# Down projection, last two blocks: 192 tokens first, then 128, with the first tokens' norm and outputs among the products

## The chip, the cores and the metric

The kernel runs on one NeuronCore of a Trainium2 chip. The metric is the device time of one execution in microseconds. Times below come from three timed runs and from one profiled execution of the kernel before; trace times are counted from the start of the profiled span.

## What is computed

One layer of a streaming encoder, for 256 prompt tokens and 64 sample tokens together (320 columns). Only its end matters here, the down projection of the feed-forward part, a norm per token, and the residual:

```python
def rmsnorm(x, g):
    y = xf * lax.rsqrt(jnp.mean(xf * xf, axis=-1, keepdims=True) + EPS)
    return (y * g).astype(x.dtype)

gate, up = jnp.split(gu, 2, axis=-1)
x = x + rmsnorm((jax.nn.silu(gate) * up) @ w_down, g_post_ffn)
```

The sum of squares of a token runs over all 2048 channels, so no output of a token can be scaled before the last of its 2048 channels is there.

## The kernel before

Channels lie on the 128 partitions and tokens along the free dimension, so the 2048 channels are 16 blocks of 128 (`KB`), numbered 0 to 15, and a block's values are a tile of 128 x 320. All float32 products are made from three products of rounded parts (type `F32R`): weight high part by activation high part, weight high by activation low, weight low by activation high. `load_split` (L218) loads a piece of weights by a DMA from SyncE's queue (L207), ScalarE rounds it to its high part `whi` (L214), and VectorE subtracts to get the low part `wlo` (L215). `whi` and `wlo` have three buffers each (`wsp`), and the loaded weights `w` three (`wst`). A cast to `whi` can start when the high-part products of three pieces before have been made; a load can start when the subtraction of three pieces before is done.

The down projection runs in four quarters of the 5632 hidden channels (`q`, L1154), each of 11 blocks of 128. For each quarter and each output block `n`, `block_matmul` (L222) takes the 11 hidden blocks as two pieces of 6 and 5 (768 and 640 weight columns): per piece the products with `gh` and `gl` (L230, L231), then the low-part products (L234). That is 33 products of 128 x 320 per block, each with its own 128 x 128 weights. Blocks 0 to 14 are added into `y` after each quarter (L1183); block 15 stays in a PSUM bank of its own through all four quarters (`held_y`, named `psy`, L1153 and L1187). In the last quarter each block's squares are added into `acc` (L1022, L1024) and `y` is multiplied by the gain (L1186).

After the last product of block 15 its squares are taken from PSUM (L1189). `rstd` (L251) adds `acc` and these squares over the partitions by products with a column of ones, which put the 320 sums on partitions (three overlapping ranges of 128 tokens, 12 records of TensorE, since plain float32 takes two passes), and takes the power -0.5 on GpSimd (L262). `rstd_rows` (L265) transposes the result back over 128 partitions (`psb`). Then the outputs follow in the order of `PLAN_Y` (L1194): VectorE multiplies one or two blocks by the row (L1220), and x is added in one of three ways: "P", two accumulating products with the identity on TensorE and a copy by ScalarE (L1150, L1229, L1230), "G" on GpSimd (L1222), "V" on VectorE (L1224). Each step ends with a DMA from SyncE's queue (L1213), in the order of the plan.

Instructions of each engine run in the order in which a scheduler laid them down at build time. `high_priority` moves instructions forward in that order, and `issue_after` ties one behind another.

Of the kernel before, what the change touches and what calls it, by code (L numbers as in the profile page):

```python
# [100 lines left out]
def trunk_kernel(ctx, tc, ins, outs):  # L101
# [1046 lines left out]
    def residual(k, pool, alone=False):  # L1148
        fin[k] = pool.tile([P, 512], F32, tag=pool.name[-1], name="fin")
        PE.matmul(fin[k][:, 0:T], cv("ident"), x1[:, k, :], start=True, stop=alone)  # L1150

    it = 0
    held_y = ps_g.tile([P, 512], F32, tag="g", name="psy")  # L1153
    for q in range(NQ):  # L1154
        gh = [act.tile([P, T], F32R, tag=f"bh{j}", name=f"gh{j}") for j in range(8)]
        for i in range(2):
# [16 lines left out]
        def gx(k):  # L1173
            return gh[k], gl[k]

        for n in range(KB - 1):
            psd = ps_p.tile([P, 512], F32, tag="p", name="psdn")
            block_matmul(psd[:, 0:T], ins["w_down"][q, n], gx, (6, 5))
            with tc.high_priority(offset=PRI_E):
                if q == 0:  # L1180
                    S.copy(y[:, n, :], psd[:, 0:T])
                else:
                    V.tensor_tensor(y[:, n, :], y[:, n, :], psd[:, 0:T], ALU.add)  # L1183
                if q == NQ - 1:
                    square_acc(n, y[:, n, :])
                    S.activation(y[:, n, :], y[:, n, :], AF.Identity, scale=pv("g4", n))  # L1186
        block_matmul(held_y[:, 0:T], ins["w_down"][q, KB - 1], gx, (6, 5), q == NQ - 1, q == 0)  # L1187
    with tc.high_priority(offset=PRI_E):
        last = square_acc(KB - 1, held_y[:, 0:T])  # L1189
        S.activation(y[:, KB - 1, :], held_y[:, 0:T], AF.Identity, scale=pv("g4", KB - 1))  # L1190
    nc.sync.dma_start(outs["ffn"], nffn)


    PLAN_Y = "P0 P1 G0809 P0203 G1011 P0405 G1213 P0607 V1415"  # L1194
    banks = [(ps_t, 0), (ps_t, 1), (ps_g, 2), (ps_g, 3), (ps_g, 4)]

    def residuals(n, mm):
        with tc.issue_after(mm.ins):
            for _ in range(n):
                pool, k = banks.pop(0)  # L1200
                residual(k, pool)

    rr, mm = rstd([acc, last], ps_p, lambda i, mm: residuals(2 * i, mm))
    rb3, mm = rstd_rows(rr, ps_p)
    residuals(3, mm)

    sent = None

    def out(k, n, sent):
        with ExitStack() as e:  # L1210
            if sent is not None:
                e.enter_context(tc.issue_after(sent.ins))
            return nc.sync.dma_start(outs["y"][:, k:k + n, :], y[:, k:k + n, :])  # L1213

    for step in PLAN_Y.split():
        how, ks = step[0], step[1:]
        n = 2 if len(ks) == 4 else 1
        k = int(ks[:len(ks) // n])
        yy = y[:, k:k + n, :]
        V.tensor_tensor(yy, yy, rb3.unsqueeze(1).to_broadcast((P, n, T)), ALU.mult)  # L1220
        if how == "G":
            G.tensor_tensor(yy, yy, x1[:, k:k + n, :], ALU.add)  # L1222
        elif how == "V":
            V.tensor_tensor(yy, yy, x1[:, k:k + n, :], ALU.add)  # L1224
        else:
            for kk in range(k, k + n):
                if kk not in fin:
                    residual(kk, (ps_t, ps_g)[kk % 2])
                PE.matmul(fin[kk][:, 0:T], cv("ident"), y[:, kk, :], start=False, stop=True)  # L1229
                S.copy(y[:, kk, :], fin[kk][:, 0:T])  # L1230
        sent = out(k, n, sent)
    pb.close()


# [79 lines left out]
```

## Time and profile before

| what | value |
|---|---|
| median of three runs | 1500.84 us (1497.14 to 1501.93) |
| profiled execution, its own time | 1498.26 us |
| its span, first to last instruction | 1496.5 us |
| outside the span | 1.76 us |
| TensorE busy, share of the span | 99% |
| weight loads (PEld) busy, share of the span | 98% |
| VectorE, ScalarE, GpSimd busy | 67%, 48%, 15% |
| mean granted TensorE clock | 0.998 |
| DMA traffic | 224.22 MB, mean 150 GB/s |

The page gives busy times per engine. TensorE's matmul ends are modelled and overlap, so the distance from one product's start to the next one's start is the better measure of its price; in a merged row of the timeline it is the row's length less one instruction's duration, divided by the count less one. A row of the timeline reads: start, length, engine, line, operation, output and inputs, shape, count, and in brackets how long the engine stood idle before it and on whom it waited.

### The profile page before, as it was taken

What the parts mean: (1) busy time and instruction counts of PE and PEld (TensorE: products, weight loads), DVE (VectorE), ACT (ScalarE), POOL (GpSimd) and SP (SyncE); (2) the same over time, 40 slices, a digit from 0 to 9 for tenths busy, and PEclk for the clock granted to TensorE, in tenths of its full rate; (3) what the DMA queues carried; (4) which work ended last, traced back from release to release, by engine and by line L of the source; (5) the groups of instructions that cost most, each with busy time, mean ns of one, the idle gap of its engine ahead of it and who ended that gap; (6) DMA issues with size and microseconds to landing.
All of it is one profiled execution on the core that took longest, in us unless ns stands there. A gap on an engine that the chain in (4) does not pass through costs nothing.

```text
span 1496.5 us, 27233 instructions
## 1 busy us (share of the span) xinstructions
PE 1480.7 (99%) x10609; PEld 1459.7 (98%) x10610; DVE 998.4 (67%) x1840; ACT 723.7 (48%) x1305; POOL 226.4 (15%) x390
## 2 busy tenths in 40 slices
PE   9999999999999999999999999999999999999998
PEld 8999899989999999999999999999999999999997
DVE  6779886979989678766335666445666545656554
ACT  7664556554544656544434444334444333444453
POOL 0011001120010000332002222002223101223101
PEclk9999999999999999999999999999999999999999
DMA  8435453444434744444554444454444455444453
GB/s 297 134 128 160 137 157 120 131 143 144 130 106 142 226 146 141 154 143 130 154 166 154 149 151 137 138 159 162 152 155 138 136 149 171 154 147 150 131 151 118
DMA packets 98281, 224.22 MB, mean 150 GB/s; under 512 B 18792, under 2 KB 39528, under 8 KB 98152
## 3 DMA queue, kind: packets, MB, share of 16 engines
q1 hardware_dynamic: 98008, 222.45, 47.4%
q8 instruction: 83, 1.36, 0.4%
q14 instruction: 46, 0.38, 0.1%
q10 hardware_dynamic: 144, 0.03, 0.0%
HBM read 215.33 MB, written 7.12 MB: 149 GB/s over the span
## 4 chain that ended last, share of the span: by engine, by line
PE 82%; DVE 9%; ACT 3%; DMA 2%; issue 2%; POOL 1%; ACTq 0%; DVEq 0%; POOLq 0%
PE psu L234 13%; PE psu L231 13%; PE psu L230 13%; PE psdn L230 7%; PE psdn L231 6%; PE psdn L234 6%; DVE wlo L215 3%; PE psq L230 3%; PE psq L231 3%; PE psq L234 3%; PE psu L1107 1%; ACT whi L214 1%; DVE cvt L560 1%; PE ps_first L395 1%; DMA w<-in_w_out 1%
## 5 line engine op out<-in xcount | busy, mean ns | idle before, releaser
L214 ACT CAST whi<-w 128x1024 fp32r<-128x1024 f32 (+2 forms) x440 | 412.9, 940 | 488.4 <-PE psu L231 169.4
L215 DVE TENSOR_TENSOR wlo<-w,whi 128x1024 fp32r<-128x1024 f32 (+2 forms) x440 | 477.3, 1085 | 196.5 <-ACT whi L214 124.7
L231 PE MATMUL psu<-lo,whi 128*128 128x320 f32 x1344 | 397.0, 309 | 0.0
L230 PE MATMUL psu<-hi,whi 128*128 128x320 f32 x1344 | 397.0, 309 | 0.0
L231 PEld LDWEIGHTS psu<-lo,whi 128*128 128x128 f32 x1344 | 252.3, 188 | 0.0
L230 PEld LDWEIGHTS psu<-hi,whi 128*128 128x128 f32 x1344 | 252.3, 188 | 0.0
L234 PE MATMUL psu<-hi,wlo 128*128 128x320 f32 x1344 | 224.4, 309 | 0.0
L234 PEld LDWEIGHTS psu<-hi,wlo 128*128 128x128 f32 x1344 | 204.0, 188 | 0.0
L231 PE MATMUL psdn<-gl,whi 128*128 128x320 f32 x660 | 195.9, 310 | 0.0
L1140 POOL COPY nffn<-fbuf 128x2 f32<-128x2 f32 x88 | 101.5, 1153 | 586.9 <-DVE fbuf L1138 583.7
L1138 DVE TENSOR_TENSOR fbuf<-psu,rb 128x256 f32<-128x256 f32 x88 | 37.4, 425 | 168.9 <-PE psu L234 168.9
L230 PE MATMUL psdn<-gh,whi 128*128 128x320 f32 x480 | 142.8, 309 | 0.0
L231 PEld LDWEIGHTS psdn<-gl,whi 128*128 128x128 f32 x660 | 123.9, 188 | 0.3
L230 PE MATMUL psq<-hh,whi 128*128 128x320 f32 x352 | 106.2, 315 | 0.0
L231 PE MATMUL psq<-hl,whi 128*128 128x320 f32 x352 | 104.1, 309 | 0.0
L230 PEld LDWEIGHTS psdn<-gh,whi 128*128 128x128 f32 x480 | 90.1, 188 | 0.0
L234 PE MATMUL psdn<-gh,wlo 128*128 128x320 f32 x480 | 89.9, 309 | 0.0
L234 PEld LDWEIGHTS psdn<-gh,wlo 128*128 128x128 f32 x480 | 75.3, 188 | 0.0
L230 PEld LDWEIGHTS psq<-hh,whi 128*128 128x128 f32 x352 | 66.1, 188 | 0.3
L231 PEld LDWEIGHTS psq<-hl,whi 128*128 128x128 f32 x352 | 66.1, 188 | 0.2
L560 DVE SCALAR_TENSOR_TENSOR cvt<-ub,par,cvt 128x320 f32<-128x320 f32 x120 | 65.3, 545 | 0.2
L1183 DVE TENSOR_TENSOR y<-y,psdn 128x320 f32<-128x320 f32 x45 | 22.0, 488 | 58.9 <-PE psdn L234 58.9
(357 smaller groups left out, 2479.5 us busy)
## 6 DMA issues: line engine op xcount, KB each, us to landing
w<-in_w_up SPq DMA_DIRECT2D x176, 512.0 KB, 3.6
w<-in_w_in SPq DMA_DIRECT2D x88, 512.0 KB, 3.9
w<-in_w_down SPq DMA_DIRECT2D x64, 384.0 KB, 3.2
w<-in_w_down SPq DMA_DIRECT2D x64, 320.0 KB, 2.9
w<-in_w_out SPq DMA_DIRECT2D x32, 320.0 KB, 3.3
w<-in_w_out SPq DMA_DIRECT2D x16, 384.0 KB, 3.1
w<-in_w_first SPq DMA_DIRECT2D x6, 512.0 KB, 6.5
wtp<-wsp SPq DMA_DIRECT2D x4, 640.0 KB, 5.8
```

The costliest lines, as they stand in the source:

```text
L214: S.copy(hi[:, 0:width], w[:, 0:width])
L215: V.tensor_tensor(lo[:, 0:width], w[:, 0:width], hi[:, 0:width].bitcast(F32), ALU.subtract)
L230: tick(PE.matmul(ps, wh, xh, start=(first and k0 + j == 0), stop=False))
L231: tick(PE.matmul(ps, wh, xl, start=False, stop=False))
L234: tick(PE.matmul(ps, lo[:, j * P:(j + 1) * P], xh, start=False, stop=(final and k0 + j == nk - 1)))
L395: tick(PE.matmul(ps, w, xh, start=(k == 0 and wt is hi), stop=(k == KB - 1 and wt is lo)))
L560: return lambda: V.scalar_tensor_tensor(acc, x, w, acc, ALU.mult, ALU.add)
L1107: PE.matmul(pss[i][:, 0:T], wt[:, o:o + P], x, start=(k == 0 and n == 0), stop=(k == KB - 1 and n == 2))
L1138: V.tensor_tensor(buf[:, 2:258], psu[:, 0:TP], rb2[:, 0:TP], ALU.mult)
L1140: G.tensor_copy(nffn[:, b, 0, :], buf[:, 256:258])
L1183: V.tensor_tensor(y[:, n, :], y[:, n, :], psd[:, 0:T], ALU.add)
```

## The change

The loop over the last quarter ends with block 13. `held_y` is gone: block 15 of the first three quarters is added into `y` like the others. For blocks 14 and 15 of the last quarter the four weight pieces are loaded and split first (`wl`), the last one into buffers of its own (`wsx`), and kept, because each is used twice: `part_products` makes the 33 products of a block for a range of tokens. The order in the program is block 14 and block 15 for tokens 0 to 191 (`ra`), then block 14 and block 15 for tokens 192 to 319 (`rz`). The sums of squares of the first tokens stand behind the 14th product of block 14's second part, and the transposes of their norm behind the 12th product of block 15's second part. Outputs are made by `out` for `ra` and then for `rz`, always two blocks at a time, eight steps each. The "P" step has one bank and two products for both blocks, 384 or 256 columns wide. The two blocks take 132 products in place of 66, 66 of them 128 x 192 and 66 of them 128 x 128. `then` ties each instruction behind the one before it on its engine; since `then` records them, most of the new instructions stand under its line, L1205.

```diff
-    held_y = ps_g.tile([P, 512], F32, tag="g", name="psy")
...
-        for n in range(KB - 1):
+        for n in range(KB if q < NQ - 1 else KB - 2):
...
-        block_matmul(held_y[:, 0:T], ins["w_down"][q, KB - 1], gx, (6, 5), q == NQ - 1, q == 0)
-    with tc.high_priority(offset=PRI_E):
-        last = square_acc(KB - 1, held_y[:, 0:T])
...
-    PLAN_Y = "P0 P1 G0809 P0203 G1011 P0405 G1213 P0607 V1415"
...
+    wsx = pb.enter_context(tc.tile_pool(name="wsx", bufs=1, reuse_waits="tile"))
+    for n in (n14, KB - 1):
+        for j0, nk in ((0, 6), (6, 5)):
+            src = ins["w_down"][NQ - 1, n][:, j0 * P:(j0 + nk) * P]
+            wl[n, j0] = load_split(src, nk * P, wsx if (n, j0) == (KB - 1, 6) else None)
...
+    def part_products(n, pool, r, between={}):
...
+                        then(PE, PE.matmul, ps[:, r], w[:, j * P:(j + 1) * P], x[j0 + j][:, r], start=first,
+                             stop=(w is lo and j0 + j == QB - 1))
...
+            then(PE, PE.matmul, fin, cv("ident"), xx, start=True, stop=False)
+            then(PE, PE.matmul, fin, cv("ident"), yy, start=False, stop=True)
+            then(S, S.copy, yy, fin)
...
+    TA = 192
+    ra, rz = slice(0, TA), slice(TA, T)
...
+    with tc.high_priority(offset=PRI_E):
+        evict(n14, part_products(n14, ps_t, ra), ra)
+        sqa = evict(KB - 1, part_products(KB - 1, ps_t, ra), ra)
+        root = []
+        evict(n14, part_products(n14, ps_p, rz, {14: lambda: root.append(row_root([acc, sqa], oa))}), rz)
+        psd = part_products(KB - 1, ps_t, rz, {12: lambda: root.append(rows(root[0], oa, ps_p))})
+        out("G0809", ra, root[1])
+        sqz = evict(KB - 1, psd, rz)
+        out("G1011", ra, root[1])
+        rr = row_root([acc, sqz], oz)
+        for step in ("P0001", "P0203"):
+            out(step, ra, root[1])
+        scale = rows(rr, oz, ps_t)
+        for step in ("G1213", "P0405", "G1415", "V0607"):
+            out(step, ra, root[1])
+        for step in ("P0001", "G0809", "P0203", "G1011", "P0405", "G1213", "G1415", "V0607"):
+            out(step, rz, scale)
```

The built order of three engines shows where this lands. Numbers behind names tell buffers apart. The first place is TensorE at the seam of blocks 12 and 13 of the last quarter. Before, block 13 (`psdn_16426`, with the first weight piece `whi_16429`) follows block 12 whole:

```order
L234 MATMUL psdn_16375<-gp1_14146,wlo_16403 128x320
L230 MATMUL psdn_16426<-gh0_14137,whi_16429 128x320
L231 MATMUL psdn_16426<-gl0_14147,whi_16429 128x320
...
L234 MATMUL psdn_16426<-gp1_14146,wlo_16454 128x320
L230 MATMUL psdn_16477<-gh0_14137,whi_16480 128x320
L231 MATMUL psdn_16477<-gl0_14147,whi_16480 128x320
```

Now, on the same engine, block 13 is `psdn_16431` (pieces `whi_16434` and, not shown, `whi_16458`), and the 192 tokens of block 14 are `psdn_16510` (pieces `whi_16488` and `whi_16494`):

```order
L234 MATMUL psdn_16380<-gp1_14151,wlo_16408 128x320
L230 MATMUL psdn_16431<-gh0_14142,whi_16434 128x320
L231 MATMUL psdn_16431<-gl0_14152,whi_16434 128x320
L1205 MATMUL psdn_16510<-gh0_14142,whi_16488 128x192
...
L1205 MATMUL psdn_16510<-gh5_14147,wlo_16489 128x192
L230 MATMUL psdn_16431<-gh1_14143,whi_16434 128x320
...
L234 MATMUL psdn_16431<-gh5_14147,wlo_16435 128x320
L1205 MATMUL psdn_16510<-gh6_14148,whi_16494 128x192
```

The first piece of block 14 (18 narrow products) stands behind two products of block 13, its second piece (15) behind block 13's first piece, and block 13's second piece comes after it.

The second place is ScalarE's casts of the last weight pieces. Before, they stand in the order of their use: `whi_16453` is block 13's second piece, `whi_16480` and `whi_16504` are block 14's, `whi_16530` and `whi_16554` block 15's:

```order
L214 CAST whi_16453<-w_16451 128x640
L214 CAST whi_16480<-w_16478 128x768
L1022 ACTIVATE sq_16422<-y_7189 128x320
L1186 ACTIVATE y_7189<-y_7189,par_81 128x320
L214 CAST whi_16504<-w_16502 128x640
L214 CAST whi_16530<-w_16528 128x768
```

Now `whi_16458` is block 13's second piece, `whi_16488` and `whi_16494` are block 14's, `whi_16500` and `whi_16506` block 15's:

```order
L214 CAST whi_16458<-w_16456 128x640
L214 CAST whi_16488<-w_16486 128x768
L1022 ACTIVATE sq_16427<-y_7189 128x320
L1185 ACTIVATE y_7189<-y_7189,par_81 128x320
L214 CAST whi_16506<-w_16504 128x640
L214 CAST whi_16494<-w_16492 128x640
L214 CAST whi_16500<-w_16498 128x768
```

Block 15's second piece, the last one loaded, has moved ahead of block 14's second piece.

The third place is the end of VectorE's program. Before, `psb_16591` is the row of the norm:

```order
L1024 TENSOR_TENSOR acc_15811<-acc_15811,sq_16524 128x320
L261 TENSOR_SCALAR rr_16588<-pst_16577 128x3
L1220 TENSOR_TENSOR y_7189<-y_7189,psb_16591 128x320 x2
L1220 TENSOR_TENSOR y_7189<-y_7189,psb_16591 128x640 x7
L1224 TENSOR_TENSOR y_7189<-y_7189,x1_6308 128x640
```

Now `psb_16647` is the row of the first 192 tokens, `psb_16699` that of the others, and `psdn_16634` the last 128-token product of block 15:

```order
L1205 TENSOR_TENSOR y_7189<-y_7189,psb_16647 128x2x192
L1205 TENSOR_TENSOR y_7189<-y_7189,psdn_16634 128x128
L1205 TENSOR_TENSOR y_7189<-y_7189,psb_16647 128x2x192
L1205 TENSOR_SCALAR rr_16684<-pst_16681 128x1
L1205 TENSOR_TENSOR y_7189<-y_7189,psb_16647 128x2x192 x6
L1205 TENSOR_TENSOR y_7189<-y_7189,x1_6308 128x2x192
L1205 TENSOR_TENSOR y_7189<-y_7189,psb_16699 128x2x128 x8
L1205 TENSOR_TENSOR y_7189<-y_7189,x1_6308 128x2x128
```

One of the eight multiplications of the first tokens stands ahead of the last eviction, seven stand behind it.

More of the change, by code (lines that the diff above doesn't have):

```diff
@@ L1197, in residuals @@
[L1197 to L1209, printed above, removed]
-        with ExitStack() as e:
-            if sent is not None:
-                e.enter_context(tc.issue_after(sent.ins))
-            return nc.sync.dma_start(outs["y"][:, k:k + n, :], y[:, k:k + n, :])
@@ L1216, in trunk_kernel, with out @@
+    TA = 192
+    ra, rz = slice(0, TA), slice(TA, T)
+    oa, oz = (0, TA - P), (T - P,)
+    sent = [None]
+    def out(step, r, scale):
         how, ks = step[0], step[1:]
```

66 lines of the change are left out of this document (53 added, 13 removed).

## The prediction

> **What bounds the kernel now.** I read the page's busy times first, then the last 30 us in stretches (span's microseconds; busy time and, in brackets, instructions of each engine; clock; DMA share; GB/s), then the timelines of the engines in them.
>
> ```profile
> span 1496.5 us, 27233 instructions
> PE 1480.7 (99%) x10609; PEld 1459.7 (98%) x10610; DVE 998.4 (67%) x1840; ACT 723.7 (48%) x1305; POOL 226.4 (15%) x390
> ```
>
> ```profile
> 1466.60:1471.40 4.80, 4.80 (x34) 4.80 (x34) 2.58 (x4) 2.56 (x5) 0.00 (x0) 1.00 0.47 149
> 1476.30:1481.10 4.80, 4.80 (x34) 4.80 (x34) 0.98 (x2) 1.04 (x2) 0.00 (x0) 1.00 0.00 0
> 1481.10:1496.50 15.40, 10.80 (x49) 7.41 (x47) 7.22 (x11) 4.26 (x10) 5.42 (x4) 0.95 0.44 170
> ```
>
> TensorE is busy without a gap up to 1481.1, and VectorE and ScalarE are idle half the time there. Behind 1481.1 lies a tail of 15.4 us in which norm, scaling and outputs have nothing to hide behind. The change wants part of that tail under products. So two prices decide: what the products of blocks 14 and 15 cost when each weight is used for 192 and then for 128 tokens, and how much of the tail really moves.
>
> **Narrow products.** First the present price (timeline of TensorE: starts of blocks 14 and 15, then six products and their weight loads in one row).
>
> ```profile
> 1471.42 0.31 PE L230 MATMUL psdn<-gh,whi 128*128 128x320 f32 x1
> 1476.26 0.31 PE L230 MATMUL psy<-gh,whi 128*128 128x320 f32 x1
> ```
>
> A block is 1476.26 - 1471.42 = 4.84 us, or 0.1467 us for each of 33 products; blocks 14 and 15 take 9.68 us. No product of this rounded kind with fewer than 320 columns is in the trace. The nearest rows are products with a full 128 x 128 load and a single column (the sums of squares, plain float32), and the weight loads by kind:
>
> ```profile
> 1480.95 0.78 PEld L256 LDWEIGHTS pst<-cst,acc 128*128 128x128 f32 x6
> 1481.79 0.74 PEld L256 LDWEIGHTS pst<-cst,sq 128*128 128x128 f32 x6
> ```
>
> ```profile
> L234 PEld LDWEIGHTS psy<-gh,wlo 128*128 128x128 f32 x32 | 5.0, 188 | 0.0
> L256 PEld LDWEIGHTS pst<-cst,acc 128*128 128x128 f32 x18 | 2.3, 190 | 0.6 <-DVE acc L1024 0.5
> ```
>
> Six loads of 0.19 us lie (0.78 - 0.19)/5 = 0.118 and (0.74 - 0.19)/5 = 0.110 us apart although each product has one column: the load sets the pace, and a rounded load lasts as long (188 ns against 190). I take 0.112 us for a narrow product, 192 or 128 columns alike. 132 x 0.112 = 14.8 us, **5.1 us more** than 9.68. The ends: every product could keep 0.1467 us (19.4 us, 9.7 more), or go by its columns (the first rival). The Trainium skill, "TensorE: Matmul & The Clock Gate", section "LDWEIGHTS (loading the stationary operand)", prices a load by its weight columns alone, about 107 ns for 128, which speaks against cutting the tokens; by it the term would be 4.4 us. The trace agrees to 5%.
>
> **Stalls.** In the new order the first piece of block 14 is wanted two products into block 13, not a block later. The present times of those weights (timelines of ScalarE, VectorE, SyncE's queue, and the loads' row of the page):
>
> ```profile
> 1466.04 0.83 ACT L214 CAST whi<-w 128x768 fp32r<-128x768 f32 x1 [1.62 <-PE psdn L231]
> 1470.88 0.83 ACT L214 CAST whi<-w 128x768 fp32r<-128x768 f32 x1 [1.62 <-PE psdn L231]
> 1468.54 0.73 ACT L214 CAST whi<-w 128x640 fp32r<-128x640 f32 x1 [0.17 <-PE psdn L231]
> ```
>
> ```profile
> 1467.18 0.95 DVE L215 TENSOR_TENSOR wlo<-w,whi 128x768 fp32r<-128x768 f32 x1
> ```
>
> ```profile
> 1465.49 3.00 SPq L207 DMA_DIRECT2D w<-in_w_down  x2
> ```
>
> ```profile
> w<-in_w_down SPq DMA_DIRECT2D x64, 320.0 KB, 2.9
> ```
>
> Block 13 starts at 1471.42 - 4.84 = 1466.58. Block 14's first piece is cast at 1466.87; with 0.19 us of signal and load its products start at 1467.06, where TensorE is ready at 1466.87: 0.2 us. Its 18 products and block 13's other 16 last to about 1471.4. Then block 14's second piece is due. Its cast stands behind that of block 15's second piece, whose load can only be issued when the subtraction at 1467.18 is over (1468.13; the second issue in the row is 1465.49 + 3.00 - 0.33 = 1468.16), and lands 2.9 us later, 1471.06. Two casts of 0.73 us and 0.19: 1472.7, a stall of 1.3 us, with all of TensorE queued behind it. Block 15's first piece takes the buffers of block 13's second piece, whose high-part products now end 0.7 us before it is wanted; as in the row at 1470.88, a cast so placed is over 0.29 us behind the block's end, with the signal 0.5 us. Sum **2.0 us**, from 1.0 (the load lands earlier) to 3. The first low part is ready at 1468.13, where its products are due at 1468.4; the others have more. The norm of the first tokens puts 8 records of 0.112 and two transposes of 0.11 between products that now run without them: **1.1 us**. Products so end 5.1 + 2.0 + 1.1 = 8.2 us later. Its power (GpSimd) has about 3 us before the transposes: no stall. The three earlier quarters now add block 15 into `y` (some 0.5 us each on VectorE or ScalarE); that lies beside products while both engines are idle 2.2 of 4.8 us, and would cost 1.5 us if it did not.
>
> **The tail.** The present one in rows:
>
> ```profile
> 1483.80 0.54 PE L269 MATMUL psb<-cst,rr 128*128 128x128 f32 x3
> 1484.18 1.78 PE L1150 MATMUL fin<-x,cst 128*128 128x320 f32 x6
> ```
>
> ```profile
> 1482.66 0.16 DVE L261 TENSOR_SCALAR rr<-pst 128x3 f32<-128x3 f32 x1 [4.68 <-PE pst L256]
> 1484.38 6.00 DVE L1220 TENSOR_TENSOR y<-y,psb 128x320 f32<-128x320 f32 x9 [1.56 <-PE psb L269]
> 1490.42 1.05 DVE L1224 TENSOR_TENSOR y<-y,x 128x640 f32<-128x640 f32 x1
> ```
>
> ```profile
> 1482.90 0.85 POOL L262 TENSOR_TENSOR rr<-rr,nhalf 128x3 f32<-128x3 f32 x1 [77.31 <-DVE rr L261]
> 1486.22 4.57 POOL L1222 TENSOR_TENSOR y<-y,x 128x640 f32<-128x640 f32 x3 [2.47 <-DVE y L1220]
> ```
>
> ```profile
> 1491.93 0.42 ACT L1230 COPY y<-fin 128x320 f32<-128x320 f32 x1 [0.65 <-PE fin L1229]
> ```
>
> ```profile
> 1492.38 0.84 SPq L1213 DMA_DIRECT2D out_y<-y  x2
> ```
>
> ```profile
> out_y<-y SPq DMA_DIRECT2D x7, 320.0 KB, 2.5
> s<-in_s_gdn SPq DMA_DIRECT2D x4, 128.0 KB, 2.8
> out_y<-y SPq DMA_DIRECT2D x2, 160.0 KB, 1.8
> ```
>
> ```profile
> 1487.80:1494.60 6.80, 4.10 (x16) 2.55 (x14) 3.64 (x5) 2.38 (x6) 2.98 (x2) 1.00 0.96 367
> ```
>
> Today the norm holds the outputs back until 1484.38, 3.3 us; the last of nine DMAs is issued at 1492.8 (11.7 us behind the products), lands 2.5 us later, and 1.2 us closes the program. With the change 3.3 us of norm do not stand before the first tokens' outputs, but only one of their eight multiplications is ahead of the last eviction. I count from the products' end. VectorE: eviction of 128 columns to 0.5, one multiplication (0.73 us per 640 columns back to back, so 0.45), the other norm's sum at 1.4, six multiplications and the "V" addition (0.65) to 5.0, eight of 256 columns (0.33) and an addition to 8.2. GpSimd, 2.4 ns per column: one addition, the power at 2 to 2.8, six more, to 8.4. TensorE makes "P" products at (1.78 - 0.43)/5 = 0.27 us per 320 columns: 0.65 for a pair of 192, 0.43 for a pair of 128; the first waits for its multiplication until 2.2, the third pair ends at 5.6, the copy 0.65 later. So the DMA of 0405 goes at 6.3, and ten follow in the plan's order, 0.84 - 0.41 = 0.43 us apart: the last at 10.6, 1.1 us earlier than now. It has 128 KB; its landing lies between 1.8 us (160 KB of the same output) and 2.8 (the 128 KB load), and I take 2.0, near the row of the same queue and direction. With the close 13.8 us against 15.4: **1.6 us less**. Ends: SyncE's queue spaced 0.55 apart because the rows are now 512 bytes, or the DMA engines, 96% busy already in the stretch above, falling behind (0.5 more than now), and a landing and close without queueing (3 less).
>
> **Sum.** 8.2 - 1.6 = 6.6 us. The profiled execution's own time is 1498.26 (span 1496.5 and 1.76 around it), so 1504.9 there; it lies 0.17% under the median of the runs shown, 1500.84, to which I add the same: **1507.4**. The three runs lie 0.3% apart, so 0.3%, 4.5 us, is about what a measurement of this kernel can tell from no change.
>
> **Rivals.** (1) Not slower: narrow products go by their columns and no load holds them. Two products of 512 columns in the trace tell the slope.
>
> ```profile
> 70.37 0.39 PE L502 MATMUL psd<-rg,strict 128*128 128x512 f32 x1
> 70.60 0.31 PE L234 MATMUL psq<-hh,wlo 128*128 128x320 f32 x1
> ```
>
> 0.23 us for 512 columns against 0.1467 for 320 is 0.43 ns per column: 0.09 us for 192, 0.063 for 128, together 10.1 us instead of 14.8. The sum falls to 1.9 us, 1502.7, within 0.3%. It decides where the mean falls under 0.096 us (6.6 - 132 x 0.016 = 4.5). Against it speak the rows at 1480.95 and 1481.79. The Trainium skill's same page, "Back-to-back issue gap", gives about 81 ns in a stream of loads and products of 128 columns; by that and 0.09 for 192 the sum is 3.1 us. No narrow rounded product is here to test it. Chance 0.13. (2) Narrow rounded products fall to the plain float32 pace, two passes of 0.27 us per 320 columns: 0.32 for 192 and 0.22 (two loads) for 128, 36 us instead of 14.8, so 1528. The trace has rounded products at 320 and 512 columns only, all at full pace; nothing shows such a step, nothing excludes it. Chance 0.12. (3) The change does more of what it says: the outputs of the first tokens drain while the others' products run, and 5 us leave the tail instead of 1.6: 1504. The order is against it, one multiplication stands early. Chance 0.07.
>
> **Chances and range.** The main case has 0.68; in it three stalls and the tail are uncertain by 2 us together, so about one in six ends within 0.3%. Slower: 0.56 + 0.12 + a part of (3) = 0.70; within: 0.12 + 0.11 + 0.04 = 0.27; faster, where (1) and (3) meet, 0.03. The range leaves out (2) and a few hundredths below: low 1502, the first rival with a slightly shorter tail; high 1512, every narrow product at 0.1467 (4.6 us above the main case).
>
> **What would show it.** Right: starts of narrow products 0.11 us apart in both parts; one stall of over 1 us of TensorE before block 14's second piece, ended by a cast; seven multiplications of the first tokens behind the last product; a tail of 13 to 14 us. Wrong: narrow products under 0.096 us or above 0.147 apart, no stall before block 14's second piece, or a tail under 11 us.

## The result and the profile after

| | median | range | executions |
|---|---|---|---|
| before | 1499.08 us | 1497.14 to 1501.93 | 6 |
| after | 1508.12 us | 1504.34 to 1514.51 | 6 |

The change makes the kernel slower: after to before 1.0066, 95% interval 1.0052 to 1.0080, that is 7.8 to 12 us. The profiled execution of the kernel after took 1504.34 us, the fastest of the six; its span is 6.1 us longer than that of before. The spread is part of the result: 10 us after, 5 us before.

The head of the page of the kernel after; TensorE's share of the span is 99%, as before.

```profile
span 1502.6 us, 27393 instructions
PE 1482.4 (99%) x10667; PEld 1460.9 (97%) x10668; DVE 1000.6 (67%) x1855; ACT 723.9 (48%) x1308; POOL 229.0 (15%) x396
```

The end of the kernel after in four stretches (busy time and instructions of the five engines, granted clock, DMA share, GB/s). Block 13 starts at 1465.94, its first stretch ends where block 14's second weight piece is due, the 192 tokens end at 1479.81, the 128 tokens at 1488.22, the rest is the tail.

```profile
1465.94:1470.75 4.81, 4.81 (x38) 4.55 (x36) 1.76 (x3) 1.78 (x4) 0.00 (x0) 1.00 0.48 148
1470.75:1479.81 9.06, 8.07 (x66) 7.65 (x64) 4.03 (x7) 3.27 (x7) 0.00 (x0) 1.00 0.00 1
1479.81:1488.22 8.41, 8.41 (x78) 8.41 (x77) 1.65 (x5) 1.53 (x4) 1.70 (x2) 1.00 0.01 2
1488.22:1502.60 14.38, 7.62 (x31) 4.85 (x30) 7.85 (x19) 3.27 (x8) 6.43 (x8) 0.88 0.58 182
```

From block 13's start to the products' end it is 22.28 us, before 1481.10 - 1466.58 = 14.52: 7.8 us more. Behind the products 14.4 us stand against 15.4. Block 13 itself started 0.64 us earlier than before, which is chance further up (the run of the kernel after again, below, shows of what kind). So 7.8 - 1.0 - 0.6 = 6.1 us, the difference of the spans. TensorE is "busy" all through the third stretch, although its products have 128 columns in place of 320: the busy share doesn't tell a thin product from a full one.

TensorE's timeline after; the count at a row's end is that of its products, the waits stand in brackets:

```profile
1467.71 0.83 PE L1205 MATMUL psdn<-gh,wlo 128*128 128x192 f32 x6
1471.71 0.35 PE L1205 MATMUL psdn<-gh,whi 128*128 128x192 f32 x1 [0.80 <-ACT whi L214]
1476.04 0.35 PE L1205 MATMUL psdn<-gh,whi 128*128 128x192 f32 x1 [0.19 <-ACT whi L214]
1479.47 0.50 PE L1205 MATMUL psdn<-gp,wlo 128*128 128x192 f32 x3
1481.34 0.55 PE L1205 MATMUL pst<-cst,acc 128*128 128x1 f32 x4
1482.20 0.64 PE L1205 MATMUL psdn<-gh,wlo 128*128 128x128 f32 x4
1485.85 0.86 PE L1205 MATMUL psdn<-gh,wlo 128*128 128x128 f32 x6
```

A row's length less one product's 0.27 or 0.28 us is five steps of 0.11 us with 192 columns (1467.71) and 0.12 with 128 (1485.85); over whole parts the starts lie 0.1115 us apart with both. The stall is the row at 1471.71: its product was due at 1470.75. ScalarE's timeline has its cause, two casts in one row behind a load that landed at 1470.31:

```profile
1470.31 1.35 ACT L214 CAST whi<-w 128x640 fp32r<-128x640 f32 x2 [2.58 <-DMA w<-in_w_down]
```

The first of the two is block 15's last piece, the second the one that TensorE waits for, as the prediction had it. The tail on VectorE, GpSimd and SyncE's queue:

```profile
1486.13 0.55 DVE L1205 TENSOR_TENSOR y<-y,psb 128x384 f32<-128x384 f32 x1 [0.62 <-PE psb L1205]
1489.61 2.86 DVE L1205 TENSOR_TENSOR y<-y,psb 128x384 f32<-128x384 f32 x6
1492.51 1.08 DVE L1205 TENSOR_TENSOR y<-y,x 128x384 f32<-128x384 f32 x1
1493.50 2.72 DVE L1205 TENSOR_TENSOR y<-y,psb 128x256 f32<-128x256 f32 x8
```

```profile
1491.21 1.95 POOL L1205 TENSOR_TENSOR y<-y,x 128x384 f32<-128x384 f32 x2 [0.39 <-issue]
1494.32 2.96 POOL L1205 TENSOR_TENSOR y<-y,x 128x256 f32<-128x256 f32 x4 [1.15 <-DVE y L1205]
```

```profile
1494.35 5.74 SPq L1274 DMA_DIRECT2D out_y<-y  x11
```

One multiplication of the first tokens stands before the products' end, seven behind it. The last DMA is issued 11.4 us behind the products' end (before 11.7). The row begins with the DMA of 0405, 6.1 us behind the products' end (6.3 in the prediction); an issue lasts 0.44 us, so the eleven lie (5.74 - 0.44)/10 = 0.53 us apart, where the prediction had taken 0.43.

### The profile page after: what moved, and what is told of

It is laid out like the page before. It is cut to its first block, busy times and chain, and to the rows that moved or that the text cites. A ratio compares the mean times of both kernels' runs of the same rounds, so it can differ in the third digit from the quotient of the medians.

```text
span 1502.6 us, 27393 instructions
## 1 busy us (share of the span) xinstructions
PE 1482.4 (99%) x10667; PEld 1460.9 (97%) x10668; DVE 1000.6 (67%) x1855; ACT 723.9 (48%) x1308; POOL 229.0 (15%) x396
## 4 chain that ended last, share of the span: by engine, by line
PE 79%; DVE 10%; ACT 4%; DMA 3%; issue 2%; POOL 1%; SPq 0%; POOLq 0%; ACTq 0%; DVEq 0%
PE psu L234 13%; PE psu L231 13%; PE psu L230 13%; PE psdn L230 7%; PE psdn L231 7%; PE psdn L234 7%; DVE wlo L215 3%; PE psq L234 2%; PE psq L230 2%; PE psq L231 2%; ACT whi L214 2%; PE psu L1107 1%; DVE cvt L560 1%; DMA w<-in_w_out 1%; DVE odd L560 1%
## 5 line engine op out<-in xcount | busy, mean ns | idle before, releaser
L231 PE MATMUL psdn<-gl,whi 128*128 128x320 f32 x682 | 202.4, 310 | 0.0
L230 PE MATMUL psdn<-gh,whi 128*128 128x320 f32 x496 | 147.6, 309 | 0.0
L231 PEld LDWEIGHTS psdn<-gl,whi 128*128 128x128 f32 x682 | 128.1, 188 | 0.3
```

Of the source, the lines that this page charges most:

```text
L230: tick(PE.matmul(ps, wh, xh, start=(first and k0 + j == 0), stop=False))
L231: tick(PE.matmul(ps, wh, xl, start=False, stop=False))
```

## The experiments

"Part" is a range of tokens (the first part the 192 tokens, the second the 128), "piece" a piece of weights. All stages below are read in the same way: from the start of the last product of the up projection (tile `psu`) to the start of the last product of the down projection, and from there to the span's end.

| kernel | to the last product | behind it | median | ratio to before, 95% |
|---|---|---|---|---|
| before | 77.72 | 15.52 | | |
| after | 85.51 | 14.45 | 1508.12 | 1.0066, 1.0052 to 1.0080 |
| after, again | 85.74 | 14.43 | 1509.43 | 1.0072, 1.0058 to 1.0086 |
| after, third | 85.58 | 15.88 | 1507.64 | 1.0062, 1.0041 to 1.0083 |
| no held block | 77.72 | 16.06 | 1498.67 | 1.0003, 0.9995 to 1.0012 |
| split alone | 84.52 | 15.45 | 1507.40 | 1.0062, 1.0049 to 1.0075 |
| casts in order | 84.66 | 15.89 | 1508.83 | 1.0062, 1.0048 to 1.0077 |
| two queues | 85.61 | 14.11 | 1504.72 | 1.0058, 1.0033 to 1.0082 |
| early rows | 88.70 | 14.35 | 1508.27 | 1.0064, 1.0046 to 1.0082 |
| second part wide | 85.51 | 14.44 | 1505.97 | 1.0044, 1.0031 to 1.0057 |
| early rows, wide | 84.87 | 12.29 | 1503.63 | 1.0033, 1.0020 to 1.0045 |
| second part 96 | 88.52 | 17.46 | 1512.01 | 1.0082, 1.0066 to 1.0099 |

**The kernel after, again.**

> The changed kernel once more, as the base for the runs beside it. Theory A (weight loads): its profile shows the same sum as the first one, products of the last three blocks 7.7 us longer than before, tail 1.0 shorter, so 5.5 to 7 us over before at an equal granted clock; executions that lie higher have a lower granted clock, and before has such executions too. Rival C (the change itself lowers the granted clock): executions of the changed kernel have a clock of 0.992 to 0.995 in about half the cases again, and before never, so that the difference of the medians is 9 us.

The stages are as in the first profile (85.74 and 14.43 us), the ratio too. Rival C's sign is there: three of these six executions have a clock of 0.992 to 0.995, and none of the 17 of the kernel before beside them lies under 0.997. But the profiled execution, 1510.29 us at 0.996, is 6 us longer than the first one with the same stages: its last product of the up projection starts at 1408.34 us and not at 1402.61. It has three stretches of 3.41 us at half clock far ahead of the change, in work that both kernels have. Their rows, and one from the profile of before:

```profile
160.54:163.96 3.42, 3.42 (x15) 3.42 (x15) 0.99 (x2) 3.37 (x11) 0.56 (x4) 0.50 0.07 23
355.10:358.52 3.42, 3.42 (x15) 3.42 (x14) 3.27 (x7) 1.62 (x6) 0.00 (x0) 0.50 0.68 170
525.77:529.18 3.41, 3.41 (x15) 3.41 (x15) 3.04 (x7) 3.17 (x7) 0.00 (x0) 0.50 0.85 249
```

```profile
160.20:163.62 3.42, 3.42 (x15) 3.42 (x14) 0.94 (x3) 3.27 (x10) 0.84 (x6) 0.50 0.12 44
```

The first profile of the kernel after has none so early. Such early stretches come in kernels with whole and with split products alike, none to three in a profile here, so a lower mean clock or a longer time of one execution is not by itself the work of the change.

**Without the held block, nothing split.** Block 15 is added into `y` in all four quarters; the rest is the kernel before.

```diff
-    held_y = ps_g.tile([P, 512], F32, tag="g", name="psy")
-        for n in range(KB - 1):
+        for n in range(KB):
-        block_matmul(held_y[:, 0:T], ins["w_down"][q, KB - 1], gx, (6, 5), q == NQ - 1, q == 0)
```

> The kernel before with one part of the change alone: block 15 is added into y in every quarter like the others, and no PSUM bank is held; products and outputs as before. Theory A: products unchanged, the tail begins with an eviction in place of squares taken from PSUM, 0.3 to 0.5 us, so before plus 0.4. Rival B (the loss sits in the three earlier quarters, where block 15 is now evicted): 2 us or more over before, spread over the starts of the quarters.

The products take 77.72 us, the same to two digits; 0.5 us is added behind them (the last eviction into `y`). The additions of the three earlier quarters are free.

**The split alone.** The products as after, the norm and the outputs as before, for all 320 tokens behind the last product.

```diff
+        evict(n14, part_products(n14, ps_t, ra), ra)
+        evict(KB - 1, part_products(KB - 1, ps_t, ra), ra)
+        evict(n14, part_products(n14, ps_p, rz), rz)
+        evict(KB - 1, part_products(KB - 1, ps_t, rz), rz)
+    PLAN_Y = "P0 P1 G0809 P0203 G1011 P0405 G1213 P0607 V1415"
```

> The changed kernel with its split products, but the norm and the outputs of all 320 tokens behind them as before. Theory A: the split costs 5.0 us for 132 weight loads 0.111 us apart and about 1.5 us of stalls, the eviction ahead of the norm 0.4, the tail is as long as before (15.4 to 15.9): 6.5 to 7.5 us over before, so the changed norm and outputs are worth about nothing in sum (1.0 spent between products, 1.0 to 1.5 gained in the tail). Rival D (products go by their columns and the loss is in the changed tail): within 2 us of before.

All of the loss is there with the split alone. Of its second part and what follows, in stretches:

```profile
1479.68:1487.02 7.34, 7.34 (x68) 7.34 (x67) 0.93 (x3) 1.53 (x4) 0.00 (x0) 1.00 0.01 2
1487.02:1502.40 15.38, 10.77 (x49) 7.44 (x48) 7.49 (x12) 4.11 (x10) 5.41 (x4) 0.92 0.44 170
```

66 products of 128 columns take 7.34 us, 0.111 us each. Against the kernel after, the sums and transposes among the products (8.41 - 7.34 = 1.07 us) are gone and the tail is 1.0 us longer: the early norm and outputs bring what they cost, and no more.

**The casts in order.** Block 15's last piece is cast behind those of block 14.

```diff
+                with tc.issue_after(cast):
+                    S.copy(hi[:, 0:width], w[:, 0:width])
+                with tc.issue_after(sub):
+                    V.tensor_tensor(lo[:, 0:width], w[:, 0:width], hi[:, 0:width].bitcast(F32), ALU.subtract)
```

> The changed kernel with the cast and the subtraction of block 15's second piece tied behind those of block 14's second piece. Theory A: the stall before block 14's second piece falls from 1.0 us to about 0.2, nothing else moves: 0.7 to 0.8 us below the changed kernel. Rival E (the stall is the freed buffer, not the place in ScalarE's queue): no change.

```profile
1472.72 0.73 ACT L214 CAST whi<-w 128x640 fp32r<-128x640 f32 x1 [2.35 <-PE psdn L231]
1473.35 0.72 ACT L1201 CAST whi<-w 128x640 fp32r<-128x640 f32 x1
```

The cast that TensorE needs now comes first and the product starts at 1473.50 with no wait recorded; the gap before block 15 stays as it was, 0.4 us. The products end 0.85 to 1.1 us sooner than in the two runs of the kernel after above: the stall and its cause are shown. The time doesn't tell it (1508.83): in the profile something in the tail took 1.4 us back, and three of the six executions have a clock of 0.993 to 0.995; that is the subject of the later runs.

**A stream of products by itself.** In the kernel before, 1,700 products are set in between blocks 14 and 15; they have a bank of their own.

```diff
+            for w, n in ((320, 100), (192, 300), (320, 100), (128, 300), (320, 100), (256, 300), (320, 100), (64, 300), (320, 100)):
+                for i in range(n):
+                    mm = PE.matmul(ps[:, 0:w], hi[:, j * P:(j + 1) * P], x[j][:, 0:w], start=(i == 0), stop=(i == n - 1))
```

> The kernel before, with a chained stream of 1,700 extra products set in at the last quarter of the down projection (128x128 weights, a new set for each product, the result is not used): 100 of 320 columns, then 300 of 192, 100 of 320, 300 of 128, 100 of 320, 300 of 256, 100 of 320, 300 of 64, 100 of 320; its output is the reference's, its time is about 200 us longer. Theory A (a product with new weights has a floor that its width does not lower): about 0.112 us from start to start at 64, at 128 and at 192 columns, 0.118 at 256, 0.147 at 320; so a token block of 320 costs 0.147 in one piece and 0.223 in any two narrow ones. Rival B (the price goes by columns, and the 0.112 after the change came from waits of that place): 0.035, 0.063, 0.09, 0.118, 0.147. For the open point of the granted clock, theory H1 (an array that waits for weights half the time draws stretches of half clock): stretches of 3.4 us at half clock inside the parts of 64 or 128 columns, none in those of 320; rival H2 (the stretches come where the engine stands idle): none in any part.

Stretches of 320, 192, 128, 256 and 64 columns (each from a width's first start to the next width's; the count in brackets includes the neighbours that reach in, 100 or 300 begin in each of the first five):

```profile
1476.93:1491.59 14.66, 14.66 (x102) 14.66 (x101) 0.98 (x2) 1.04 (x2) 0.00 (x0) 1.00 0.01 1
1491.59:1525.07 33.48, 33.48 (x303) 33.48 (x301) 0.00 (x0) 0.00 (x0) 0.00 (x0) 1.00 0.00 1
1539.76:1573.21 33.45, 33.45 (x303) 33.45 (x301) 0.00 (x0) 0.00 (x0) 0.00 (x0) 1.00 0.00 1
1587.93:1623.53 35.60, 35.60 (x303) 35.60 (x301) 0.00 (x0) 0.00 (x0) 0.00 (x0) 1.00 0.00 1
1638.20:1641.50 3.30, 3.30 (x33) 3.30 (x31) 0.00 (x0) 0.00 (x0) 0.00 (x0) 0.99 0.00 0
1641.50:1699.07 57.57, 57.57 (x272) 57.57 (x272) 0.00 (x0) 0.00 (x0) 0.00 (x0) 0.50 0.00 1
```

The price is 0.1466 us at 320 columns, 0.1187 at 256, 0.1116 at 192, 0.1115 at 128 and 0.11 at 64: a product with new weights has a floor that its width does not lower. That the load is what sets it fits the one-column rows of the prediction, but every product here brings a load, so this isn't tested apart. The stream settles the first two rivals. The Trainium skill's figure of about 81 ns ("TensorE: Matmul & The Clock Gate", section "Back-to-back issue gap") isn't reached by these rounded float32 products at any width. The last row is new: 3.3 us after the products of 64 columns have begun the granted clock falls to half and a product takes 0.213 us, with no gap on TensorE.

**Three outputs on ScalarE's queue.**

```diff
+            if r is rz and k in (4, 6, 14):
+                nc.scalar.dma_start(outs["y"][:, k:k + n, r], yy)
```

> The kernel after, with three of the last eight output transfers (blocks 4 and 5, 6 and 7, 14 and 15 of the 128 tokens) issued by ScalarE's queue in place of SyncE's. Theory A (at the end SyncE's queue, at 0.54 us a transfer, sets the last issue): the last issue comes about 1.0 to 1.6 us earlier, and the time from the last down product to the end falls from 14.4 to about 13. Rival B (the engines that make the outputs, or the landing of the transfers, set the end): no change over 0.4 us there. The time as a whole stays above that of the kernel before by 4 to 9 us with both.

SyncE's and ScalarE's queues in that run:

```profile
1488.57 10.62 SPq L1277 DMA_DIRECT2D out_y<-y  x13
```

```profile
1498.05 1.60 ACTq L1275 DMA_DIRECT2D out_y<-y  x3
```

The last issue ends 10.7 us behind the products (at 1499.65, the products at 1488.94), 1.2 us earlier than in the kernel after (1500.09 and 1488.22: 11.9), but the end comes only 0.3 us earlier. Rival B: the transfers themselves end the program. The stretches of the tails say why. Before, the DMA engines were busy 0.44 of 15.40 us, 6.8 us; after, 0.58 of 14.38, 8.3 us, for the same 2.62 MB. In pieces of 768 and 512 bytes a row the outputs go at 314 GB/s of busy time, in rows of 1280 bytes at 386 (the size of a transfer changes with the row, so the two aren't separated). From 1496 to 1501 the DMA engines are 0.92 busy in the kernel after and 0.97 in the run with two queues.

**Early rows.** Casts in order, the first tokens' statistics at the 9th and 18th product of block 14's second part, and five of their eight output steps ahead of the last eviction.

```diff
+        evict(n14, part_products(n14, ps_p, rz, {9: lambda: root.append(row_root([acc, sqa], oa)), 18: early_rows}), rz)
+        psd = part_products(KB - 1, ps_t, rz)
+        early("V0203", "G1213")
```

> The kernel after, with two edits: the last weight piece is cast after those of block 14 (as in the run with the casts in order), and the statistics of the first 192 tokens are taken at the 9th and 18th product of block 14's second part, so that five of their eight output steps are done before the last products end. Theory A (the stall before 14b costs 0.8 to 1.0 us, and the outputs of the first tokens that stand behind the last product cost 2 to 3 us): the products end 0.8 to 1.0 us sooner, and the time behind them falls from 14.4 to about 12.4 us; in sum 2.5 to 3.5 us under the kernel after, and still 4 to 6 us above the kernel before, since the 5 us of the narrow products stay. Rival B (what stands behind the last product is set by the chain of the last 128 tokens alone): the time behind the last product stays within 0.5 us of 14.4. Rival C (outputs beside the products slow them): the products' starts go over 0.115 us apart, and the gain of the tail is given back.

None of the theories foresaw what its profile has. Four stretches of the second part:

```profile
1478.75:1482.16 3.41, 3.41 (x33) 3.41 (x32) 1.17 (x4) 0.95 (x3) 0.00 (x0) 1.00 0.00 0
1482.16:1485.58 3.42, 3.42 (x32) 3.31 (x31) 0.89 (x3) 0.62 (x2) 0.74 (x2) 1.00 0.00 0
1485.58:1493.85 8.27, 8.27 (x41) 8.27 (x41) 4.19 (x8) 0.71 (x2) 2.95 (x3) 0.50 0.36 121
1493.85:1499.23 5.38, 4.98 (x13) 3.19 (x13) 2.60 (x8) 1.19 (x3) 1.55 (x2) 0.50 0.00 0
```

From 1485.58 to 1499.23, four times 3.41 us, TensorE has half its clock; the narrow products there are 0.213 us apart. The stretch of 3.41 us just before is the one that holds the sums of the first tokens: eight records with one column, two transposes and 19 products of 128 columns, some 2,700 columns in all. That gives theory H1: the clock of a stretch is set by how many columns the stretch before it had. The next runs test it.

**Other widths.** The same stream with 600 products of 128 columns, then 300 each of 112, 96 and 80.

> The kernel before with the extra stream again (chained products with new 128x128 weights, result not used, the kernel's output is the reference's), now 100 of 320 columns, 600 of 128, 100 of 320, 300 of 112, 100 of 320, 300 of 96, 100 of 320, 300 of 80, 100 of 320. In the first stream the products of 64 columns (27 ns of columns in 109 ns, a quarter of the time) drew the clock to half 3.3 us after they began, and those of 128 columns (53 of 111.5, a half) ran 33 us at full clock. Theory H1 (the gate looks at how much of a stretch of 3.4 us the array computes, not at whether the engine waits): between a quarter and a half lies a bound; 128 columns keep full clock for 67 us, 80 (0.30) draw half clock, 96 (0.36) most likely too, 112 (0.42) is open; half clock costs 0.213 us a product. Rival H2 (the half clock at 64 columns came by chance of that moment): no half clock in this stream, 0.11 us throughout.

```profile
1491.50:1558.44 66.94, 66.94 (x602) 66.94 (x601) 0.00 (x0) 0.00 (x0) 0.00 (x0) 1.00 0.00 1
1573.17:1606.61 33.44, 33.44 (x303) 33.44 (x301) 0.00 (x0) 0.00 (x0) 0.00 (x0) 1.00 0.00 1
1621.35:1625.90 4.55, 4.55 (x44) 4.55 (x42) 0.00 (x0) 0.00 (x0) 0.00 (x0) 1.00 0.00 0
1625.90:1681.11 55.21, 55.21 (x262) 55.21 (x260) 0.00 (x0) 0.00 (x0) 0.00 (x0) 0.50 0.00 1
1701.00:1757.45 56.45, 56.45 (x266) 56.45 (x266) 0.00 (x0) 0.00 (x0) 0.00 (x0) 0.50 0.00 1
```

128 columns (67 us) and 112 (33 us) keep the full clock, 96 and 80 lose it after 4.5 and 3.9 us and don't get it back before the products of 320 columns return. In columns per 3.41 us at 0.1115 us a product: 3,400 are enough, 2,900 are not. A pure stream of 128 columns (3,900) is safe, the same stream with eight one-column sums and two transposes in it (2,700) is not.

**The second part wide.** The last 128 tokens' products take 192 columns, 64 of them again; their sums are not used.

```diff
+        m = slice(min(r.start, T - TA), r.stop)
-                        then(PE, PE.matmul, ps[:, r], w[:, j * P:(j + 1) * P], x[j0 + j][:, r], start=first,
+                        then(PE, PE.matmul, ps[:, m], w[:, j * P:(j + 1) * P], x[j0 + j][:, m], start=first,
```

> The kernel after, with one edit: the products of the last 128 tokens take 192 columns of the block (64 of them again, their sums are not used), so that the array computes 0.72 of the time and not 0.48. Theory H1 (the part of the loss that goes with a lower granted clock comes from half-clock stretches in the products of 128 columns and the one-column sums among them): products still 0.112 us apart, stages as in the kernel after (products end 22.3 us after block 13's start, 14.4 us behind them), granted clocks back at 0.998 to 1.000 as in the kernel before, median 1504 to 1506, ratio 1.004 to 1.005. Rival H2 (the stretches come in the tail) or H3 (chance upstream): clocks spread from 0.992 to 0.999 as in the kernel after, median about 1508. Rival A (products go by columns): the part costs 66 x 0.027 = 1.8 us more.

```profile
1482.27:1490.73 8.46, 8.46 (x78) 8.46 (x77) 1.65 (x5) 1.53 (x4) 1.70 (x2) 1.00 0.01 2
1490.73:1505.10 14.37, 7.60 (x31) 4.81 (x29) 7.88 (x19) 3.27 (x8) 6.45 (x8) 0.91 0.58 182
```

Half again as many columns cost nothing (8.46 us against 8.41). The median lies 1.7 us under that of the kernel after on the same chip (1507.64, below); the two intervals overlap, so the times alone don't settle it. The clocks say more: 0.996 to 0.999 here, not quite the 0.998 and above that H1 expected, against 0.992 to 0.998 in those runs of the kernel after.

**Early rows with the second part wide.** Both edits.

> The kernel of the run with early rows, with the wide second part: last weight piece cast in order, first tokens' statistics at the 9th and 18th product, five output steps of the first tokens ahead of the last eviction, the last part's products 192 columns wide. With H1 the clock stays at 0.998 or above, so that the tail is seen undisturbed: theory A says 12.4 us behind the last product (14.4 in the kernel after), products 21.2 to 21.5 us from block 13's start, median about 1502.5, still 3.5 to 4.5 us above the kernel before; rival B (the chain of the last 128 tokens sets the tail): 14.0 to 14.4 us behind the last product, median about 1504.

```profile
1480.93:1489.54 8.61, 8.61 (x78) 8.50 (x77) 5.20 (x11) 1.53 (x4) 2.73 (x3) 1.00 0.15 46
1489.54:1501.70 12.16, 6.31 (x27) 4.14 (x25) 5.23 (x15) 2.79 (x7) 5.53 (x7) 0.89 0.59 184
```

The clock holds through the products, and with it the tail is 12.3 us, as theory A had it. This is the best of the split versions, 1503.63 us, and still slower than the kernel before by 3.0 to 6.7 us; the forecast of 1502.5 was 1.1 us too low.

**The kernel after, a third time.**

> The kernel after once more, for runs on the same chip as the two above. Median 1506 to 1509, clocks from 0.992 to 0.999. If its profile falls on an execution of low clock, H1 expects the half-clock stretches in the products of the last 128 tokens or right behind their statistics, H2 in the tail, H3 upstream of 1400.

Here the profile fell on an execution with a half-clock stretch near the end:

```profile
1490.26:1493.67 3.41, 2.86 (x24) 2.61 (x23) 1.32 (x5) 0.71 (x2) 1.50 (x2) 1.00 0.17 58
1493.67:1497.09 3.42, 3.42 (x7) 1.80 (x6) 3.38 (x7) 0.48 (x1) 2.98 (x4) 0.50 0.17 58
```

It begins at 1493.67, behind a stretch that holds the last 16 narrow products, four one-column records and the wait for the squares. That is H2's place, and its price is read from the tail: 15.88 us against 14.43 to 14.45, 1.4 us. The run with the casts in order had the same (15.89). H1's cause is not shown for it: by their starts the products of the stretch before have 2,820 columns, and a stretch of the second run, likewise the one with the last narrow products, with 2,819 columns and as much idle time, was followed by full clock. So was the stretch behind the last product of the kernel before, with 2,314 columns:

```profile
1491.74:1495.16 3.42, 2.87 (x27) 2.78 (x26) 1.31 (x3) 0.42 (x2) 1.00 (x1) 1.00 0.13 45
1495.16:1498.57 3.41, 3.41 (x12) 1.93 (x13) 3.05 (x8) 0.94 (x3) 2.92 (x4) 1.00 0.23 79
```

```profile
1481.16:1484.57 3.41, 3.41 (x22) 2.62 (x21) 0.35 (x2) 0.85 (x2) 0.85 (x1) 1.00 0.00 0
1484.57:1487.99 3.42, 3.42 (x15) 2.29 (x14) 3.42 (x6) 1.21 (x3) 1.77 (x2) 1.00 0.04 14
```

All three stretches hold products of plain float32, which take two passes, so a count of columns alone does not rank them. H3 has its part too: the same profile has a half-clock stretch at 524.28, and its last product of the up projection starts 3.8 us later than in the first profile.

**The second part at 96 columns.** All but the first product of each chain take 96 columns; the other 32 tokens' sums are left out.

```diff
+                        m = r if first or r is ra else slice(r.start, r.start + 96)
-                        then(PE, PE.matmul, ps[:, r], w[:, j * P:(j + 1) * P], x[j0 + j][:, r], start=first,
+                        then(PE, PE.matmul, ps[:, m], w[:, j * P:(j + 1) * P], x[j0 + j][:, m], start=first,
```

> The kernel after, with one edit: in the products of the last 128 tokens all but the first of each chain take 96 columns (the other 32 tokens' sums are left out). By columns that would be 64 products less 13 ns, 0.9 us saved; by the load's floor nothing. Theory H1 (the gate goes by the share of time in which the array computes, and its bound lies between 0.36 and 0.42): here 0.36 of the time, so half clock begins 3 to 7 us after the second part has begun, in every execution or nearly; products then 0.213 us apart, the clock at 0.993 or below, and with 7 to 10 us of the products and up to 6 us of the tail in it the median is 1511 to 1516. Rival H3 (the low clocks of the kernel after are chance): as the kernel after, 1507 to 1509, clocks from 0.992 to 0.999. Rival A (columns set the price): 1507 or less.

```profile
1484.71:1489.80 5.09, 5.09 (x48) 5.09 (x47) 0.80 (x3) 0.86 (x3) 0.70 (x1) 1.00 0.00 0
1489.80:1496.13 6.33, 6.33 (x32) 6.33 (x32) 0.85 (x2) 0.68 (x2) 1.00 (x1) 0.50 0.10 34
1496.13:1503.40 7.27, 6.90 (x15) 4.15 (x16) 4.95 (x11) 1.58 (x4) 3.47 (x4) 0.50 0.16 54
```

Less work is slower: 1512.01 us. The half clock begins 5.1 us after the second part and holds for four stretches; the products end 3.0 us later than in the kernel after and the tail is 3.0 us longer. All six executions have clocks of 0.992 to 0.995.

## Why the prediction was right, and where it was not

**The narrow products** (5.1 us): right. 0.1115 us at both widths, 132 x 0.1115 = 14.7 us, 5.0 more than 9.68. The stream by itself shows that it is a floor of products with new weights and not the place. Rival 1 (by columns, 1502.7) and rival 2 (plain float32 pace, 1528) fall with it.

**The stalls** (2.0 us): the mechanism was right, the size 0.4 us too high. 0.15 us before block 14's first piece, 1.0 before its second (1470.75 to 1471.71), 0.4 before block 15: some 1.6. The one before the second piece was put at 1.3; the load that the cast waits for landed at about 1470.3, 4.4 us after block 13's start and not 4.5, the two casts took 1.35 us back to back where 1.46 was taken, and the product followed after 0.05 us where 0.19 was taken. Ordering the casts removes all but 0.2 us of it.

**Statistics among the products** (1.1 us): right, 1.07 us by the split alone.

**The tail** (-1.6 us): the sign was right, the size was -1.0. The step that failed is "ten follow in the plan's order, 0.84 - 0.41 = 0.43 us apart: the last at 10.6": the DMA of 0405 went at 6.1 (6.3 forecast), but the issues behind it were 0.53 us apart, so the last was at 11.4. The landing and the close took 3.0 us where 3.2 was taken. The spacing lay in the bounds given (0.55 for the queue, and the DMA engines falling behind), but the value taken was the one of long rows, and the two-queue run shows that both ends were at work: with the queue relieved the DMA engines set the end. A second row was off: the "V" addition took 1.08 us where 0.65 was taken. Rival 3 (outputs drain beside products) fell as predicted for the order that the change has; where the order is changed so that they do, in the run with early rows and a wide second part, the tail is 12.3 us, 3.2 and not 5 under the one before.

**The sum and the forecast.** The stages of undisturbed executions give 5.0 + 1.6 + 1.1 - 1.0 = 6.7 us against 6.6 predicted. The forecast of 1507.4 us lies 0.7 us from the median of 1508.12, but it came so close by luck, through two errors of opposite sign. It was added to the median of three runs, 1500.84; that of six is 1499.08. And it lacked a term: over its 17 executions the kernel after has a mean granted clock of 0.9955, the kernel before, over 45 in the runs that measured the experiments, 0.9985. Twice the difference of 0.0030 times 1507 us is 9 us more at half clock in an execution. Some 1.7 us of them cost nothing: in the first profiles the clock is at half for the last 3.4 us of the span after and the last 1.7 us before, where TensorE has no work left. The other 7.3 us are 2.1 stretches of 3.41 us; at 1.4 to 1.5 us each (the tail of the third run; the early rows, where four stretches cost 3.8 us in the products and 2.1 in the tail against the run with the wide second part) that is about 3 us, an estimate. 6.7 + 3 = 9.7, where the three intervals of the kernel after together reach from 6.1 to 12.9 us.

**What is shown of that term, and what isn't.** Shown: thin products lower the clock though TensorE never waits (both streams); with 96 columns all six executions of the kernel have a clock of 0.995 or less, with 192 none of ten fell to 0.995, with 128 seven of 17 did; a stretch in the tail of the kernel after itself. Not seen: the four stretches inside the second part in a profile of the kernel after itself, as its three profiles fell on executions without them. They were seen in the run with early rows, whose second part is as narrow and has the same sums, but there the two transposes fall into the same stretch as the sums; in the kernel after they come 31 products later. The likeliest reading is that such stretches make the five executions at 0.992 and 0.993 (1510.9 to 1514.5 us): none of the 45 of the kernel before lies under 0.996, and the profiled run with 96 columns, four such stretches and two early ones, has 0.992 too. For the two at 0.995 (1508.6 and 1509.6 us) the early stretches are enough, as the second profile shows. Whether such stretches come would then depend on where the stretches' grid falls against the sums: in the first profile the stretch with all eight sums (1478.72 to 1482.13) still held nine products of 192 columns and had 3,500 columns in all, in the third run one with 3,080 kept the clock, and in the early rows the sums fell into one without any of 192. Of 31 records in a stretch, eight sums leave 23 products of 128, some 2,950 columns at least, about what the stream of 96 columns had when it lost the clock. What lowers the clock in those executions of the kernel after itself stays open, as no profile here caught one.

## What to carry to other kernels

Cutting the moving side of a product below the floor that new weights set (here 0.11 us, reached at 192 columns) doesn't make it cheaper: price both halves at that pace, and subtract only then what the overlap brings. Before moving a tail under products, count which queue and which row length the outputs will have, since the smaller pieces here cost DMA time that the tail was short of already. And a thin product can have a second price beside its own: look at the granted clock over several executions, not only at the profile of the fastest.

## What the hardware showed that was not expected

- **The clock falls without any idle time.** Streams of 64, 80 and 96 columns with new 128 x 128 weights ran at half clock from 3.3, 3.9 and 4.5 us after their start on, for 17 to 18 stretches of 3.41 us, and regained it 3 to 5 us into products of 320 columns; 112 and 128 columns didn't. The Trainium skill, "TensorE: Matmul & The Clock Gate", section "HAM oscillation — how this bites in real kernels", gives the rule as no idle gaps of TensorE above some 3.4 us; the streams had none at all and lost the clock all the same. Its window of 3,413 ns that runs freely (Part 1 of that page, section "What's actually happening") agrees with the 3.41 us of the traces. The bound is known only roughly, for pure streams between 96 and 112 columns: with plain float32 and idle time in the stretch, 2,819 columns kept the clock in one run and 2,820 lost it in another.
- **VectorE's addition waits for GpSimd's.** The addition of 384 columns at 1492.51 ended at 1493.59, 0.43 us behind GpSimd's additions (1491.21 + 1.95 = 1493.16), while the multiplications by the row in PSUM beside them kept their 0.46 us. In the run with early rows and a wide second part the same addition took 0.56 us where GpSimd stood idle (at 1488.79) and 1.07 where it was adding (at 1485.46). The Trainium skill, "SBUF — State Buffer", section "SBUF: two separate sides", has it so: an operation of VectorE with two inputs in SBUF and one of GpSimd shut each other out for the whole instruction. The trace agrees.
